# Writing the third group's products of 64 columns into the other two groups' output banks

## The chip, the cores and the metric

The kernel runs on one core of one Trainium2 chip. The metric is the device time of one execution in microseconds, from its first to its last instruction. Four compute engines work on their own queues: TensorE (PE, with its weight loads listed as PEld), VectorE (DVE), ScalarE (ACT) and GpSimd (POOL). SyncE (SP) issues the transfers. Each queue is executed in order, and a semaphore holds an instruction until what it needs is there.

## The reference, cut to what matters

Two layers over 1024 tokens of width 1024: a gated linear attention layer, then a layer in which 8 query heads attend over one shared set of keys and values in three groups. A group is a window and a dilation; the three results are mixed by a softmax over their log sums, gated with `silu(g)`, and projected.

```python
SWA_GROUPS = ((128, 1), (512, 4), (2048, 16))
for gi, (window, dilation) in enumerate(SWA_GROUPS):
    o_g, lse_g = dilated_window_attention(q[:, :, gi], k_sh[:, :, gi], v_sh[:, :, gi], window, dilation)
wts = jax.nn.softmax(jnp.stack(lses, axis=0), axis=0)
o = jnp.sum(wts[..., None] * jnp.stack(outs, axis=0), axis=0)
x = layer_norm(DEEPNORM_ALPHA * x + (o * jax.nn.silu(g)) @ w_out)
```

With dilation 16 and 1024 tokens, the third group splits the tokens into 16 residues of 64 tokens each, and each residue attends only within itself. The change concerns the last step of this group: probabilities times values, and the sum with the other two groups.

## The kernel before, in words

The kernel is written against a recording layer. Every call such as `S.tensor.matmul` is recorded (`record`, line 162), and `order` (line 254) then plays a list schedule: at each step it takes, over all engines, the recorded operation that could start earliest, with ties going to the order of the program. The durations it plays with come from its own function `cost` (lines 543 to 595). They set the order in which instructions stand in the queues and nothing else. For a TensorE product of plain float32 that function has these lines:

```python
        if n >= 128:
            return 4 * n / 2400 + 0.009
        if args[1].shape[0] == 64:
            return 0.12
        m = args[1].shape[1]
        return {32: 0.02, 64: 0.05}.get(m, 0.43)
```

`n` is the number of output columns and `m` that of the weights. Since all instructions are issued in one place, the profile gives line 452 for nearly all of them, and one goes by the names of the tiles.

The second layer (`layer_b`, line 1176) works on 8 units, one query head each. For a unit `u`, `q_proj` makes the queries of the three groups, `scores` makes masked scores (tile `lv`), exponentials (`P`) and their row sums, `g_proj` makes the gate (`sg`), `attend` multiplies with the values, and `close` applies the gate and stores the result `og`. Between the units' instructions stand those of the projections (tile `acc`: three products of 512 columns for each of 8 blocks of the contraction). Units 0 to 3 have their gate before `attend` and are closed right after it; units 4 to 6 are closed later, after `g_proj` at line 1531; unit 7 has its gate first and is attended last, while the output projection already runs.

In `attend`, every probability tile `P` is scaled by the mixing weights `cw`. Then, for the third group, four transposes go to a tile `ms` (4 blocks of 128x128), and four copies put 64x64 blocks into two block-diagonal tiles `diag` (lines 1457 to 1461). Eight products of 128 columns (value block as weights, `diag` block moving) fill two PSUM tiles named `po`. Four copies of DVE bring these in token order into `og`. Two more `po` tiles, from the same two buffers, then take the products of the second group (12) and the first (15), whose probabilities `turn` transposes and masks (tiles `PT`, four buffers); an output element of the second group steps by 4 columns. Two additions bring `po` and `og` together.

TensorE in plain float32 needs two instructions for one product here: the profile counts 128 matmuls and 128 weight loads for the 64 products `po<-diag,V` of the 8 units. PSUM has two buffers each for `acc`, `lv`, `ms` and `po`.

Of the kernel before, what the change touches and what calls it, by code (L numbers as in the profile page):

```python
# [7 lines left out]
F32 = mybir.dt.float32  # L8
# [589 lines left out]
def trunk(tc, xT, wP, wA, wA12, wAv3, w2, wO, wK, wV0, wV12, wB, wOB, par_d,  # L598
          ident_d, lmask_d, cos_d, sin_d, bmask_d, rmask_d, tri_d, lnr_d, out):
    S = Sched(tc, lat=LAT, pad=PAD)  # L600
# [4 lines left out]
    ps = S.pool("ps", space="PSUM")  # L605
# [12 lines left out]
    def page(pool, dt, name):  # L618
        return pool.tile([128, T], dt, name=name, tag="pg", bufs=16)

    def hs(half):
        return slice(half * 512, half * 512 + 512)
# [65 lines left out]
    def blk(x, j):  # L688
        return x[:, j * 128:j * 128 + 128]
# [363 lines left out]
    def small(name, tag, bufs, dt=F32, shape=(128, 512)):  # L1053
        return hp.tile(list(shape), dt, name=name, tag=tag, bufs=bufs)
# [121 lines left out]
    def layer_b(xs, early):  # L1176
# [117 lines left out]
        U = [dict() for _ in range(8)]  # L1294
# [5 lines left out]
        def column(g, j):  # L1300
            return 8 + j % 2 * 4 + j // 2 if g == 1 else g * 8 + j
# [19 lines left out]
        def pieces(P, g, j0):  # L1321
            p, o = P[g, j0 + 1]
            n = 1 if g or not j0 else 2
            v = p[:, o + 256 - n * 256:o + 256].rearrange("p (a two b) -> p a two b", a=n, two=2)
            return v[:, :, 0], v[:, :, 1]
# [89 lines left out]
        def attend(u):  # L1415
            P, cw, Vc = U[u]["P"], U[u]["cw"], V[u // 4]
            og = page(p0, F32, "og")
            U[u]["og"] = og

            def turn(g, j0):  # L1420

                own, prev = (small("PT", "d", 4).rearrange("p (a b) -> p a b", a=4) for _ in range(2))
                pt = ps.tile([128, 4, 128], F32, name="ms", bufs=2)
                def has(x):
                    return x.rearrange("p (a two) b -> p a two b", two=2)[:, :, 1] if g else x[:, 0 if j0 else 1:]

                with S.group():
                    for i in range(4):
                        p, o = P[g, j0 + i]
                        S.tensor.transpose(pt[:, i, :], blk(p[:, o:], BL[g][j0 + i][2] // 128 - 1), ident)  # L1430

                for i in (0, 2):
                    front = pieces(P, g, j0 + i)[0]
                    n = front.shape[1]
                    S.vp.tensor_mul(prev[:, i + 2 - n:i + 2], front, ident[:, None, :].to_broadcast([128, n, 128]))
                S.vector.tensor_mul(own, pt, upto.to_broadcast([128, 4, 128]))
                S.vector.copy_predicated(has(prev), below.to_broadcast(list(has(prev).shape)), has(pt))
                return own, prev


            x = P[2, 0][0].rearrange("p (j k q) -> p k j q", j=4, k=2)
            w = cw[:, 16:24].rearrange("p (k j one) -> p k j one", k=2, j=4)
            S.vector.tensor_mul(x, x, w.to_broadcast([128, 2, 4, 64]))
            for g in (1, 0):
                for j in range(8):
                    p, o = P[g, j]
                    x = p[:, o:o + BL[g][j][2]]
                    S.vap.scale(x, x, cw[:, column(g, j):column(g, j) + 1])

            p = P[2, 0][0]
            pt = ps.tile([128, 4, 128], F32, name="ms", bufs=2)
            with S.group():
                for i in range(4):
                    S.tensor.transpose(pt[:, i, :], blk(p, i), ident)
            for k in range(2):
                h = slice(k * 64, k * 64 + 64)
                for s in range(2):
                    (S.scalar.copy if s else S.vector.tensor_copy)(  # L1460
                        diag[s][h].rearrange("p (j k q) -> p j k q", j=4, k=2)[:, :, k, :], pt[h, :, s * 64:s * 64 + 64])
            po = [ps.tile([128, 512], F32, name="po", bufs=2) for _ in range(2)]
            with S.group():
                for s in range(2):
                    for j in range(4):
                        x = s * 4 + j
                        S.tensor.matmul(po[s][:, j * 128:j * 128 + 128], blk(Vc[2], x), blk(diag[s], j),
                                         start=True, stop=True)
            for s in range(2):
                for k in range(2):  # L1470
                    x = s * 8 + k * 4
                    S.vector.tensor_copy(
                        og.rearrange("p (n a e) -> p n a e", n=8, a=8)[:, :, :, x:x + 4],
                        po[s].rearrange("p (j k a n) -> p k n a j", j=4, k=2, a=8)[:, k])
            po = [ps.tile([128, 512], F32, name="po", bufs=2) for _ in range(2)]
            started = [False, False]

            def pv(bank, outv, vblk, rhs, last=False):
                S.tensor.matmul(outv, vblk, rhs, start=not started[bank], stop=last)
                started[bank] = True  # L1480


            for r0 in (0, 2):
                own, prev = turn(1, 2 * r0)
                for r in (r0, r0 + 1):
                    i = 2 * (r - r0)
                    ov = [po[i].rearrange("p (i r) -> p r i", r=4)[:, r, :] for i in range(2)]
                    pv(0, ov[0], blk(Vc[1], 2 * r), own[:, i, :])
                    pv(1, ov[1], blk(Vc[1], 2 * r), prev[:, i + 1, :])
                    pv(1, ov[1], blk(Vc[1], 2 * r + 1), own[:, i + 1, :])  # L1490

            for n0 in (0, 4):
                own, prev = turn(0, n0)
                for i in range(4):
                    n = n0 + i
                    out_n = po[n // 4][:, i * 128:i * 128 + 128]
                    if n:
                        pv(n // 4, out_n, blk(Vc[0], n - 1), prev[:, i, :])
                    pv(n // 4, out_n, blk(Vc[0], n), own[:, i, :], last=(i == 3))

            for i in range(2):
                S.vector.tensor_add(og[:, hs(i)], po[i], og[:, hs(i)])

        def close(u):
            og, sg = U[u]["og"], U[u]["sg"]
            for i in range(2):
                S.vector.scalar_tensor_tensor(og[:, hs(i)], og[:, hs(i)], 0.5, sg[:, hs(i)],
                                              op0=OP.mult, op1=OP.mult)
            if u < 6:
                S.sync.dma_start(ogB[u], og)  # L1510

        diag = [small("diag", "a", 13) for _ in range(2)]
# [3 lines left out]
        for u in range(8):  # L1516
            scores(u)
            if u < 4:
                g_proj(u)
            if u + 1 < 8:  # L1520
                q_proj(u + 1)
            if u < 7:
                attend(u)
                if u < 4:
                    close(u)
            if u == 3:
                reload_kv()
        for u in (4, 5, 6, 7):
            if u == 7:
                early()  # L1530
            g_proj(u)
            if u < 7:
                close(u)
        attend(7)
        close(7)
        return U

# [29 lines left out]
    U = layer_b(x1s, early)  # L1567
# [118 lines left out]
```

## Time and profile before

| | before |
|---|---|
| three runs, median (lowest to highest) | 1153.4 us (1152.9 to 1153.89) |
| profiled execution: span, the only time its page gives | 1152.7 us |
| PE, PEld busy | 1142.8 us, 975.2 us |
| DVE, ACT, POOL busy | 820.3, 449.1, 188.0 us |
| matmuls and weight loads | 7780 and 7780 |
| granted TensorE clock | 0.998 |

The profiled execution lies 0.7 us below the median of the runs. A row of a group gives its shape, the count, the busy time, the mean of one, and the idle time of the engine ahead of it with what ended most of it. A row of the timeline gives start, length, the engine, and how many instructions of one name follow each other. The length of a matmul in the profile contains a pipeline latency, so what a matmul costs a busy TensorE is the distance from one start to the next.

### The profile page before, as it was taken

To read this page: it belongs to the slowest core of one execution; us is meant where nothing else is said; L and a number is where in the kernel's file an instruction comes from. 1 tells how busy PE (TensorE), PEld (TensorE's weight loads), DVE (VectorE), ACT (ScalarE), POOL (GpSimd) and SP (SyncE) were. 2 spreads that over 40 slices of the span, in tenths; PEclk is the share of its full clock that TensorE was granted. 3 is DMA by queue.
4 is the path that set the end of the run, shared out by engine and by line. 5 is a ranking of instruction groups with operands and counts; after the bars stand their busy time and mean duration, and the time that the engine had idled before them with its cause. 6 is when DMAs were issued, how large, how long until landed. Compare 5 with 4: busy or idle time off the path is not lost.

```text
span 1152.7 us, 19731 instructions
## 1 busy us (share of the span) xinstructions
PE 1142.8 (99%) x7780; PEld 975.2 (85%) x7780; DVE 820.3 (71%) x1634; ACT 449.1 (39%) x929; POOL 188.0 (16%) x139
## 2 busy tenths in 40 slices
PE   9999999999999999999999999999999999999997
PEld 9888888889988888888988888888888888888876
DVE  6286862786966699764366868686777878767678
ACT  5355431646463335311214242424222443444342
POOL 1000100112011120211020303030211312212200
PEclk9999999999999999999999999999999999999999
DMA  7211222111144365443611111121141111134544
GB/s 256 71 38 38 74 79 87 38 61 51 57 171 140 137 214 158 166 143 103 208 47 34 51 38 57 38 50 45 38 165 39 38 21 38 39 96 126 193 136 182
DMA packets 93372, 108.39 MB, mean 94 GB/s; under 512 B 43648, under 2 KB 61952, under 8 KB 93280
## 3 DMA queue, kind: packets, MB, share of 16 engines
q1 hardware_dynamic: 93280, 107.13, 29.6%
q8 instruction: 61, 1.00, 0.4%
q14 instruction: 31, 0.25, 0.1%
HBM read 85.94 MB, written 21.17 MB: 93 GB/s over the span
## 4 chain that ended last, share of the span: by engine, by line
PE 93%; DVE 4%; DMA 2%; ACT 1%; issue 1%; POOL 0%; DVEq 0%; ACTq 0%
PE acc L452 63%; PE po L452 9%; PE lv L452 8%; PE vac L452 7%; PE ms L452 4%; PE pro L452 2%; DMA wf<-in_wOB 2%; DVE rt L452 1%; DVE wl L452 1%; DVE x1l L452 0%; ACT wh L452 0%; DVE P L452 0%; DVE lnA L452 0%; ACT woh L452 0%; DVE wol L452 0%
## 5 line engine op out<-in xcount | busy, mean ns | idle before, releaser
L452 PE MATMUL acc<-x1h,wh 128*128 128x512 f32 x608 | 252.3, 415 | 0.0
L452 PE MATMUL acc<-x1h,wl 128*128 128x512 f32 x608 | 237.6, 391 | 0.0
L452 PE MATMUL acc<-x1l,wh 128*128 128x512 f32 x608 | 237.1, 390 | 0.0
L452 ACT ACTIVATE wh<-wf 128x1024 fp32r<-128x1024 f32 (+2 forms) x104 | 108.1, 1040 | 281.0 <-PE acc L452 194.8
L452 POOL TENSOR_TENSOR wl<-wf,wh 128x1024 fp32r<-128x1024 f32 x39 | 93.5, 2397 | 553.1 <-ACT wh L452 414.8
L452 ACT ACTIVATE P<-P,sts 128x128 f32<-128x128 f32 (+2 forms) x192 | 81.5, 426 | 139.6 <-DVE sts L452 139.3
L452 PEld LDWEIGHTS acc<-x1h,wl 128*128 128x128 f32 x608 | 114.1, 188 | 24.5
L452 PEld LDWEIGHTS acc<-x1l,wh 128*128 128x128 f32 x608 | 114.5, 188 | 21.3
L452 PEld LDWEIGHTS acc<-x1h,wh 128*128 128x128 f32 x608 | 114.4, 188 | 21.1
L452 DVE TENSOR_TENSOR wl<-wf,wh 128x1024 fp32r<-128x1024 f32 (+2 forms) x66 | 83.4, 1265 | 58.2 <-ACT wh L452 48.0
L452 PE MATMUL acc<-xh,wh 128*128 128x512 f32 x256 | 101.8, 397 | 0.0
L452 PE MATMUL acc<-xh,wl 128*128 128x512 f32 x256 | 99.8, 390 | 0.0
L452 PE MATMUL acc<-xl,wh 128*128 128x512 f32 x256 | 99.7, 390 | 0.0
L452 DVE TENSOR_TENSOR t<-acc,cosT 128x512 f32<-128x512 f32 x60 | 41.4, 689 | 65.7 <-PE acc L452 65.7
L452 DVE TENSOR_TENSOR t<-acc,sinT 64x512 f32<-64x512 f32 x120 | 82.5, 688 | 1.6
L452 PE MATMUL lv<-K,Q 128*64 128x64 f32 (+2 forms) x512 | 70.2, 286 | 0.0
L452 DVE CUSTOM_DVE_ANT_0 P<-lv,bmask 128x256 f32<-128x256 f32 (+1 forms) x128 | 46.7, 379 | 25.1 <-PE lv L452 23.7
L452 PEld LDWEIGHTS lv<-K,Q 128*128 128x128 f32 (+1 forms) x512 | 53.8, 163 | 10.0 <-issue 1.6
L452 PE MATMUL acc<-ogh,wh 128*128 128x512 f32 x152 | 60.1, 395 | 0.0
L452 PE MATMUL acc<-ogh,wl 128*128 128x512 f32 x152 | 59.2, 389 | 0.0
L452 PE MATMUL acc<-ogl,wh 128*128 128x512 f32 x152 | 59.2, 389 | 0.0
L452 PEld LDWEIGHTS acc<-xh,wl 128*128 128x128 f32 x256 | 48.0, 188 | 10.2
(252 smaller groups left out, 2233.4 us busy)
## 6 DMA issues: line engine op xcount, KB each, us to landing
wf<-in_wB SPq DMA_DIRECT2D x32, 512.0 KB
wf<-in_wA SPq DMA_DIRECT2D x24, 512.0 KB
wf<-in_wO SPq DMA_DIRECT2D x16, 512.0 KB
wf<-in_wOB SPq DMA_DIRECT2D x16, 512.0 KB
wf<-in_wV SPq DMA_DIRECT2D x12, 512.0 KB
res<-in_xT SPq DMA_DIRECT2D x16, 256.0 KB
x1d<-rt SPq DMA_DIRECT2D x16, 256.0 KB
out<-rt SPq DMA_DIRECT2D x16, 256.0 KB
```

The costliest lines, as they stand in the source:

```text
L452: getattr(handle[o.eng], meth)(*[conv(a) for a in args], **{k: conv(v) for k, v in kw.items()})
```

## The change: what it does

The two `po` tiles are allocated once per unit. Each product of the third group is split by token halves, so that 16 products of 64 columns take the place of 8 of 128, and each writes straight to the places of its tokens in the bank that the other two groups add into. The output of one product has three strides: 2 residues 4 columns apart, 8 places 16 columns apart, and 4 blocks 128 columns apart, the last varying fastest. The first of these products starts the bank; all later ones add. The four copies from `po` to `og` and the two additions are gone. `close` reads `po` where the gate is there already (units 0 to 3 and 7); in units 4 to 6 two copies on ACT bring `po` to `og` first.

```diff
             po = [ps.tile([128, 512], F32, name="po", bufs=2) for _ in range(2)]
-            with S.group():
-                for s in range(2):
-                    for j in range(4):
-                        x = s * 4 + j
-                        S.tensor.matmul(po[s][:, j * 128:j * 128 + 128], blk(Vc[2], x), blk(diag[s], j),
-                                         start=True, stop=True)
-            for s in range(2):
-                for k in range(2):
-                    x = s * 8 + k * 4
-                    S.vector.tensor_copy(
-                        og.rearrange("p (n a e) -> p n a e", n=8, a=8)[:, :, :, x:x + 4],
-                        po[s].rearrange("p (j k a n) -> p k n a j", j=4, k=2, a=8)[:, k])
-            po = [ps.tile([128, 512], F32, name="po", bufs=2) for _ in range(2)]
             started = [False, False]
...
+            with S.group():
+                for i in range(2):
+                    ov = po[i].rearrange("p (n a s k j) -> p s j k a n", n=4, a=8, s=2, k=2)
+                    for s in range(2):
+                        for j in range(4):
+                            d = blk(diag[s], j).rearrange("p (k a n) -> p k a n", k=2, a=8)
+                            pv(i, ov[:, s, j], blk(Vc[2], s * 4 + j), d[:, :, :, i * 4:i * 4 + 4])
...
-            for i in range(2):
-                S.vector.tensor_add(og[:, hs(i)], po[i], og[:, hs(i)])
+            if "sg" not in U[u]:
+                for i in range(2):
+                    S.scalar.copy(og[:, hs(i)], po[i])
+                po = None
+            U[u]["po"] = po
...
-                S.vector.scalar_tensor_tensor(og[:, hs(i)], og[:, hs(i)], 0.5, sg[:, hs(i)],
+                S.vector.scalar_tensor_tensor(og[:, hs(i)], po[i] if po else og[:, hs(i)], 0.5, sg[:, hs(i)],
```

Over the whole program TensorE has 128 products of 64 columns for 64 of 128, and otherwise the same ones; DVE has 32 copies `og<-po` and 16 additions less; ACT has 6 copies `og<-po` more; the number of transfers is the same. The planner's `cost` takes its branch for fewer than 128 columns, so it books 0.43 for each of the 16 products where it booked 0.222 for each of the 8. From the first such group on, the order of the queues is therefore another.

The first place is TensorE in unit 0, from the third group's products on (`po<-diag,V`). The transposes `ms` that follow are those of the next turns; `lv<-K,Q 64x64` are scores of the next unit. Before:

```order
L452 MATMUL po<-diag,V_5481 128x128 x8
L452 MATMUL ms<-ident,P 128x128 x8
L452 MATMUL lv<-K_5174,Q 64x64 x16
L452 MATMUL po<-PT,V_5401 128x128 x2
L452 MATMUL lv<-K_5008,Q 128x128
L452 MATMUL po<-PT,V_5401 128x128 x10
L452 MATMUL ms<-ident,P 128x128 x4
```

With the change, same place:

```order
L452 MATMUL po<-diag,V_5481 128x2x8x4 x16
L452 MATMUL po<-PT,V_5401 128x128 x6
L452 MATMUL ms<-ident,P 128x128 x8
L452 MATMUL lv<-K_5174,Q 64x64 x16
L452 MATMUL lv<-K_5008,Q 128x128
L452 MATMUL acc<-x1h_4373,wh 128x512
L452 MATMUL acc<-x1l_4390,wh 128x512
L452 MATMUL acc<-x1h_4373,wl 128x512
L452 MATMUL po<-PT,V_5401 128x128 x6
L452 MATMUL po<-PT,V_4656 128x128 x7
```

The first six products of the second group now stand directly behind those of the third, ahead of the transposes and scores.

The second place is TensorE in unit 5. Before, six triples of `acc` and two pairs of `lv` stood between the third group's products and the eight transposes; with the change:

```order
L452 MATMUL acc<-x1h_4351,wh 128x512
L452 MATMUL acc<-x1l_4362,wh 128x512
L452 MATMUL acc<-x1h_4351,wl 128x512
L452 MATMUL po<-diag,V_7898 128x2x8x4 x16
L452 MATMUL ms<-ident,P 128x128 x8
L452 MATMUL lv<-K_7888,Q 64x64 x16
L452 MATMUL lv<-K_7886,Q 128x128
L452 MATMUL acc<-x1h_4373,wh 128x512
L452 MATMUL acc<-x1l_4390,wh 128x512
L452 MATMUL acc<-x1h_4373,wl 128x512
L452 MATMUL po<-PT,V_7896 128x128 x12
```

The transposes of the second group's probabilities now follow the products at once; the projection's triples are ahead of the products instead.

The third place is DVE in the same unit with the change, from the scaling of the third group's tile on. `TENSOR_SCALAR P<-P,cw` scales the first and second groups' tiles, which those eight transposes read.

```order
L452 TENSOR_TENSOR P<-P,cw 128x2x4x64
L452 TENSOR_TENSOR t_8764<-acc,cosT 128x512
L452 TENSOR_TENSOR t_8771<-acc,sinT 64x512 x2
L452 COPY diag<-ms 64x4x64 x2
L452 TENSOR_TENSOR Q<-t_8764,t_8771 128x4x8x16
L452 TENSOR_SCALAR P<-P,cw 128x128
L452 TENSOR_SCALAR P<-P,cw 128x256 x5
L452 TENSOR_SCALAR P<-P,cw 128x128 x3
L452 TENSOR_SCALAR P<-P,cw 128x256
L452 TENSOR_TENSOR PT<-P,ident 128x128 x2
L452 TENSOR_TENSOR PT<-ms,upto 128x512
L452 COPY_PREDICATED PT<-below,ms 128x2x128
```

Before, the four copies `og<-po` stood ahead of the scalings, of which DVE had seven; now the copies are gone and DVE has ten.

More of the change, by code (lines that the diff above doesn't have):

```diff
@@ L1499, in attend, with close @@
                     pv(n // 4, out_n, blk(Vc[0], n), own[:, i, :], last=(i == 3))
-            for i in range(2):
-                S.vector.tensor_add(og[:, hs(i)], po[i], og[:, hs(i)])
-        def close(u):
-            og, sg = U[u]["og"], U[u]["sg"]
-            for i in range(2):
-                S.vector.scalar_tensor_tensor(og[:, hs(i)], og[:, hs(i)], 0.5, sg[:, hs(i)],
+            if "sg" not in U[u]:
[3 more added lines that the diff above has]
+            U[u]["po"] = po
+        def close(u):
+            og, sg, po = (U[u][n] for n in ("og", "sg", "po"))
+            for i in range(2):
+                S.vector.scalar_tensor_tensor(og[:, hs(i)], po[i] if po else og[:, hs(i)], 0.5, sg[:, hs(i)],
                                               op0=OP.mult, op1=OP.mult)
```

## The prediction, made before the run

> **What bounds the kernel now.** First the page's head and its chain of waits, then what TensorE waited for in all.
>
> ```profile
> span 1152.7 us, 19731 instructions
> PE 1142.8 (99%) x7780; PEld 975.2 (85%) x7780; DVE 820.3 (71%) x1634; ACT 449.1 (39%) x929; POOL 188.0 (16%) x139
> PE 93%; DVE 4%; DMA 2%; ACT 1%; issue 1%; POOL 0%; DVEq 0%; ACTq 0%
> PE pro L452 <- DVE Dg L452: 1.2, 1, 1.2
> PE po L452 <- DVE PT L452: 0.8, 1, 0.8
> PE ms L452 <- DVE sum L452: 0.5, 2, 0.2
> PE ms L452 <- ACT sum L452: 0.2, 1, 0.2
> ```
>
> TensorE is busy 99% of the span and 93% of the chain. The last four lines are all its waits (total, times, longest): 2.7 us, of which 0.8 lies in the stage of the change. So the 820 us of DVE are hidden: work taken from DVE can win back those 0.8 us and no more, and each microsecond put on TensorE lengthens the kernel. The stretches of units 0 and 5, in the columns stretch, PE, PEld, DVE, ACT, POOL, clock, DMA:
>
> ```profile
> 654.80:715.70 60.90, 60.90 (x347) 52.30 (x346) 45.23 (x119) 21.36 (x68) 13.14 (x12) 1.00 0.17 45
> 946.00:996.00 50.00, 50.00 (x307) 43.27 (x306) 40.32 (x122) 21.45 (x77) 13.46 (x11) 1.00 0.16 34
> ```
>
> In unit 0 DVE has 15.7 us to spare, in unit 5 only 9.7. TensorE is without a gap in both, at full clock, and DMA does little.
>
> **What the change removes.**
>
> ```profile
> L452 DVE COPY og<-po 128x256 f32<-128x256 f32 x32 | 11.8, 418 | 2.1 <-PE po L452 1.5
> L452 DVE TENSOR_TENSOR og<-po,og 128x512 f32<-128x512 f32 x16 | 11.0, 690 | 6.0 <-PE po L452 5.9
> L452 ACT ACTIVATE th<-acc 128x512 f32<-128x512 f32 x16 | 9.4, 588 | 20.6 <-PE acc L452 20.6
> ```
>
> DVE loses 11.8 us of copies and 11.0 us of additions; ACT gains 6 copies of 512 columns at about 0.59 us (third row, same size and source), 3.5 us on an engine 39% busy. Behind TensorE's queue this is worth nothing, with one exception in unit 7:
>
> ```profile
> 1052.89 1.40 DVE L452 COPY og<-po 128x256 f32<-128x256 f32 x4
> 1054.95 3.13 PE L452 MATMUL po<-PT,V 128*128 128x128 f32 x24 [0.77 <-DVE PT L452]
> ```
>
> There the four copies stand ahead of the masks that TensorE waits 0.77 us for. Without them this gap closes: -0.8 us.
>
> **What it adds to TensorE.** The 64 products become 128 of half the columns: the same 8192 columns, twice the instructions and weight loads.
>
> ```profile
> 654.83 1.95 PE L452 MATMUL po<-diag,V 128*128 128x128 f32 x16
> 656.61 1.04 PE L452 MATMUL ms<-ident,P 128*128 128x128 f32 x8
> 657.58 1.15 PE L452 MATMUL lv<-K,Q 128*64 128x64 f32 x32
> 658.66 0.71 PE L452 MATMUL po<-PT,V 128*128 128x128 f32 x4
> ```
>
> From 654.83 to 656.61 the 16 instructions of the 8 products take 1.78 us, 0.111 each. No row shows a full set of weights followed by only 64 columns, so that price has to be bounded. Streaming alone gives half of 0.111, 0.056. The 64-column scores have 64 weight columns and alternate between the two halves of the array: 32 in 1.08 us (657.58 to 658.66), 16 per half, 0.067 each. What speaks for more is the weight load:
>
> ```profile
> L452 PEld LDWEIGHTS lv<-X 128*32 128x32 f32 x1536 | 16.5, 110 | 3.0 <-issue 2.8
> L452 PEld LDWEIGHTS lv<-K,Q 128*64 128x64 f32 x256 | 8.1, 138 | 2.3 <-issue 1.6 <-DVE zz L452 0.7
> L452 PEld LDWEIGHTS po<-diag,V 128*128 128x128 f32 x128 | 15.4, 191 | 0.7 <-issue 0.2
> L452 PE MATMUL po<-PT,V x432: 270/275/377, 658.7 to 1065.5; 128*128 128x128 f32 x144
> ```
>
> Load lengths grow with the weight columns, 110, 138, 191 ns for 32, 64, 128: from 64 to 128 that is 53 ns for 64 columns, so 128 columns take about 107. The last row says the same from the other side: a `po` product is 270 ns at least, and 377 at most. The longest is the one at 658.66 that finds its weights not loaded (the load starts with it): 107 ns more. So two such loads can't follow each other closer than about 107 ns, and while the load of one product can run under another of 128 columns (both about 107, hence 0.111), it can't hide under 53 ns of streaming. I take 0.111 for the new instruction too: a product of 64 columns costs what one of 128 does. The ends are 0.056 and, if load and streaming did not overlap at all, 107 + 53 = 0.160.
>
> Sum: 32 x 0.111 = 3.56 us per unit for 1.78, +1.78, and +14.2 us over 8 units, all on the bounding engine. The ends give 1.79 us (+0.1 in all) and 5.12 us (+27).
>
> The strided output is the other unknown. The second group writes with steps of 4 columns, the first without:
>
> ```profile
> 659.43 2.40 PE L452 MATMUL po<-PT,V 128*128 128x128 f32 x20
> 664.39 3.29 PE L452 MATMUL po<-PT,V 128*128 128x128 f32 x28
> ```
>
> Without the 0.275 of the last one, 19 steps take 2.13 us and 27 take 3.02: 0.112 each. A step of 4 costs nothing; one of 128 is not shown, but half the columns in the same 0.111 leave it twice the time per column. I take nothing. [...]
>
> **What the new order adds.** In unit 0, TensorE goes from the third group straight to six products of the second. Their masked tile is the one made by
>
> ```profile
> 654.35 0.45 DVE L452 COPY_PREDICATED PT<-below,ms 128x256 f32<-128x256 uint8 x1
> ```
>
> done at 654.80, while TensorE gets there at 654.83 + 3.56 = 658.4. The later steps follow alike: transposes until 659.7 + 0.9, masks 1.1 us behind the first four of them at 661.4, wanted (after 16 score products, one more and a triple) at 662.6. Units 0 to 3 have slack. Units 4 to 6 have less. Unit 5 before:
>
> ```profile
> 943.97 0.60 PE L452 MATMUL ms<-ident,P 128*128 128x128 f32 x4
> 946.47 1.95 PE L452 MATMUL po<-diag,V 128*128 128x128 f32 x16
> 953.70 1.03 PE L452 MATMUL ms<-ident,P 128*128 128x128 f32 x8
> 946.67 0.69 DVE L452 TENSOR_TENSOR t<-acc,cosT 128x512 f32<-128x512 f32 x1 [0.16 <-PE acc L452]
> 947.38 1.39 DVE L452 TENSOR_TENSOR t<-acc,sinT 64x512 f32<-64x512 f32 x2
> 950.68 1.13 DVE L452 TENSOR_TENSOR Q<-t,t 128x512 f32<-128x512 f32 x1
> 951.74 3.25 DVE L452 TENSOR_SCALAR P<-P,cw 128x128 f32<-128x128 f32 x7
> 648.37 1.16 DVE L452 TENSOR_SCALAR P<-P,cw 128x128 f32<-128x128 f32 x5
> ```
>
> The eight transposes came 7.2 us behind the third group's products, with projections between; now they stand directly behind. Count from the four transposes (943.97 here, call it 0): 0.4 for them, five triples of 0.68 and 3.56 bring TensorE to the eight transposes at 7.3. DVE must have scaled their sources by then: 0.3 until the projection's last product is through, 0.69 + 1.39 for its rotation, 0.86 for two copies to `diag` (0.43 each), 1.1 for `Q`, then ten scalings at 0.46 (the row of seven) or 0.23 (the row of five): 9.0 or 6.6. TensorE waits 1.7 us or not at all; I take 0.8. Unit 6 has the same order, unit 4 one triple less and a DVE queue as full: 3 x 0.8 = +2.4 us, between 0 and 5.1. Behind those transposes stand the next unit's scores, so nothing else fills the wait.
>
> Total: 14.2 + 2.4 - 0.8 = +15.8, a span of 1168.5 us. The runs' median lies 0.7 above the span before: **1169 us**, +1.4%.
>
> **The rivals.**
>
> *The load hides after all, and DVE's relief counts.* If the array takes a new load while the last is still waiting, an instruction costs 0.056 to 0.067: 1.79 to 2.14 us per unit, +0.1 to +2.9 in all. If DVE, free of the copies, also scales at 0.23 in units 4 to 6, no wait appears, and with -0.8 the kernel is not slower: 1152.7 to 1155.5, say 1154. For it: three lengths of weight loads are latencies, and loads do run in pairs in the 64-column scores. Against it: the 377. It decides up to 0.058 per instruction: 8 x (32 x 0.058 - 1.78) = +0.6. [...]
>
> *The load hides, but the order makes TensorE wait.* At 2 us for the products TensorE reaches the eight transposes at 5.8, DVE at 6.6 to 9.0 as before: 0.8 to 3.2, 2 us in each of three units, +6, with +1.5 for the products and -0.8: 1160.
>
> *Short runs or wide steps cost.* The moving block is read in runs of 4 columns, the output written 128 apart. At 0.160 per instruction: +27 - 0.8, without waits since TensorE is late: 1180; more if it is worse. For it: no row has these patterns. Against it: the step of 4 that cost nothing.
>
> **How the numbers follow.** Load-bound, as summed: 68%; its own range is 1165 (no waits: 14.2 - 0.8, or 0.109 per instruction) to 1174 (5.1 of waits and as much again in unit 7). Hidden load with waits 14%, hidden without 8%, wide steps 10%. Two in ten left out gives 1157 to 1178. This kernel can't be told from no change within 0.2%, 2.3 us. Faster needs the second case and more than 0.8 us from elsewhere, which the 2.7 us of waits hardly hold: 2%. Within 0.2%: most of the hidden load without waits, 6%. Slower: 92%.
>
> **What would show it.** Right: the groups of 32 instructions `po<-diag,V` take 3.5 to 3.6 us from first start to the next instruction, weight loads 107 to 112 ns apart; units 0 to 3 last 62.7 instead of 60.9 us; the waits of PE name `ms` or `po` behind DVE's `P` or `PT` with 0 to 5 us; the 0.77 of unit 7 is gone; DVE has some 20 us less. Wrong: a group of 1.8 to 2.1 us (the load hides), or of 5 us and more (steps cost); waits in units 0 to 3, or over 2 us in a unit.

## The result and the profile after

The changed kernel takes 1167.9 us (1167.71 to 1168.49) against 1153.64 us (1152.9 to 1155.78) for the kernel before, run beside it: a ratio of 1.0122, with a 95% interval of 1.0108 to 1.0137. It is slower by 14.3 us. First the head of the page after, with its chain of waits, and all waits of TensorE (total, times, longest):

```profile
span 1166.7 us, 19927 instructions
PE 1157.0 (99%) x7908; PEld 991.6 (85%) x7908; DVE 799.7 (69%) x1602; ACT 449.2 (38%) x929; POOL 175.0 (15%) x129
PE 96%; DVE 3%; ACT 1%; issue 0%; DVEq 0%; ACTq 0%
PE pro L452 <- DVE Dg L452: 1.2, 1, 1.2
PE ms L452 <- ACT P L452: 0.5, 1, 0.5
PE ms L452 <- DVE sum L452: 0.2, 1, 0.2
PE ms L452 <- ACT sum L452: 0.2, 1, 0.2
```

The span grew by 14.0 us and TensorE's busy time by 14.2 (1142.8 to 1157.0). DVE lost 20.6 us (820.3 to 799.7) and POOL 13.0 (188.0 to 175.0; the planner moved some of its work to DVE), and nothing of that shortened the span: TensorE was already busy 99% of it. Its waits went from 2.7 to 2.1 us. The timeline of TensorE in unit 0, from the third group's products on, and the stretches from one such group to the next (stretch, PE, PEld, DVE, ACT, POOL, clock, DMA):

```profile
655.48 3.68 PE L452 MATMUL po<-diag,V 128*128 128x64 f32 x32
659.00 1.56 PE L452 MATMUL po<-PT,V 128*128 128x128 f32 x12
655.48:718.22 62.74, 62.74 (x363) 54.16 (x362) 42.43 (x113) 20.91 (x68) 13.21 (x12) 1.00 0.17 44
718.22:780.96 62.74, 62.74 (x363) 54.15 (x362) 42.40 (x113) 21.03 (x68) 13.19 (x12) 1.00 0.17 44
```

The 32 instructions take 3.51 us (655.48 to 659.00), where 16 took 1.78: +1.73 us. Units 0 and 1 last 62.74 us each; the stretch shown of before lasted 60.90. So of the 1.84 us that a unit lost, 1.73 are the products. Eight groups make +13.9 us (from the starts before rounding). The clock is 1.00, and TensorE has no gap.

### The profile page after: what moved, and what is told of

Its sections match the earlier page's. It is cut to its first block, busy times and chain, and to the rows that moved or that the text cites. A ratio compares the mean times of both kernels' runs of the same rounds, so it can differ in the third digit from the quotient of the medians.

```text
span 1166.7 us, 19927 instructions
## 1 busy us (share of the span) xinstructions
PE 1157.0 (99%) x7908; PEld 991.6 (85%) x7908; DVE 799.7 (69%) x1602; ACT 449.2 (38%) x929; POOL 175.0 (15%) x129
## 4 chain that ended last, share of the span: by engine, by line
PE 96%; DVE 3%; ACT 1%; issue 0%; DVEq 0%; ACTq 0%
PE acc L452 63%; PE po L452 10%; PE lv L452 10%; PE vac L452 7%; PE ms L452 4%; PE pro L452 2%; DVE rt L452 1%; DVE wl L452 1%; DVE x1l L452 0%; ACT P L452 0%; DVE lnA L452 0%; ACT wh L452 0%; DVE diag L452 0%; ACT diag L452 0%; DVE sum L452 0%
## 5 line engine op out<-in xcount | busy, mean ns | idle before, releaser
L452 POOL TENSOR_TENSOR wl<-wf,wh 128x1024 fp32r<-128x1024 f32 x38 | 91.1, 2397 | 549.0 <-ACT wh L452 397.0
L452 DVE TENSOR_TENSOR Q<-t,t 128x512 f32<-128x512 f32 x43 | 57.5, 1336 | 1.3
```

The lines of the kernel that those rows point to most:

```text
L452: getattr(handle[o.eng], meth)(*[conv(a) for a in args], **{k: conv(v) for k, v in kw.items()})
```

## The experiments

Three questions were open: what sets the price of a narrow product, what the new order costs, and what the relief of DVE is worth. The first had three theories: the weight load of 128 columns, the steps and short runs of the new pattern, or a fixed price per instruction.

### The split alone, in place

```diff
-    S.tensor.matmul(po[s][:, j * 128:j * 128 + 128], blk(Vc[2], x), blk(diag[s], j), ...)
+    for c in (j * 128, j * 128 + 64):
+        S.tensor.matmul(po[s][:, c:c + 64], blk(Vc[2], x), diag[s][:, c:c + 64], ...)
```

The planner's booking of the halves was halved too, so that the queues keep the order of before.

> The kernel before, with one thing changed: each product of the third group is made as two of 64 adjacent columns into adjacent columns of the bank it wrote before. The copies, the additions and the order of the queues stay, and there is no step in any output. Load theory (an instruction costs the load of 128 weight columns, 0.110 us, whatever it streams up to 128 columns): the 32 instructions of a unit take 3.5 us instead of 1.78, +1.73 x 8 = +13.8, time 1167.4 us, and the wait of 0.77 us in unit 7 stays. Pattern theory (64 columns stream in 0.055 us, and only the runs of 4 columns and the steps of 4, 16 and 128 of the changed kernel made it 0.110): 32 x 0.055 = 1.8 us a unit, time 1153.5 us.

Measured: 1167.73 us, ratio 1.0124 (1.0107 to 1.0140). Its timeline of TensorE in unit 0:

```profile
655.27 3.68 PE L452 MATMUL po<-diag,V 128*128 128x64 f32 x32
658.79 1.04 PE L452 MATMUL ms<-ident,P 128*128 128x128 f32 x8
```

Again 3.52 us, with adjacent columns on both sides, copies and additions in place and the old order. The split alone gives the whole loss of the changed kernel; the pattern theory (1153.5) falls. One thing in the expectation was wrong: the wait of unit 7 did not stay. That is taken up below.

### Half as many weight columns

```diff
+    for m in (0, 64):
         ...
-        S.tensor.matmul(po[s][:, c:c + 64], blk(Vc[2], x), diag[s][:, c:c + 64], ...)
+        S.tensor.matmul(po[s][m:m + 64, c:c + 64], Vc[2][:, x * 128 + m:x * 128 + m + 64], diag[s][:, c:c + 64], ...)
```

> As the split in place, but each of the 64-column products is made twice with 64 weight columns each, first all with the lower half of the value columns, then all with the upper half: 64 instructions a unit, each with a load and a stream half as long as before. Load theory: a load of 64 columns is about 54 ns (138 - 191 ns against 128 columns in the profile before), the stream of 64 columns 53 ns, so 0.055 each, 64 x 0.055 = 3.5 us a unit, time again about 1167.4 us. Theory of a fixed price (any instruction of plain float32 needs 0.110 us, and the weights have nothing to do with it): 64 x 0.110 = 7.0 us a unit, +5.25 x 8 = +42, time 1195.5 us.

Measured: 1169.68 us, ratio 1.0143 (1.0127 to 1.0158). Its timeline in unit 0:

```profile
655.28 3.77 PE L452 MATMUL po<-diag,V 128*64 128x64 f32 x64
658.98 1.09 PE L452 MATMUL ms<-ident,P 128*128 128x128 f32 x8
```

Now 64 instructions take 3.70 us, 0.058 each: the same 64 streamed columns cost half when the weights have half the columns. So there is no fixed price of 0.11, which would have given 1195.5 us. The load sets the price. (The expectation had 0.055; the 0.003 more is most of the 2 us above its 1167.4.)

### The same number of instructions with 128, 64 and 32 columns

Three kernels issue 64 instructions per unit in the third group, all with 128 weight columns: `repeat_128` makes each of the old products four times, `repeat_64` each half twice, `quarters` splits into four of 32 columns.

```diff
     # quarters
-    S.tensor.matmul(po[s][:, j * 128:j * 128 + 128], ..., blk(diag[s], j), ...)
+    for c in range(j * 128, j * 128 + 128, 32):
+        S.tensor.matmul(po[s][:, c:c + 32], ..., diag[s][:, c:c + 32], ...)
```

> As the split in place, but into four products of 32 adjacent columns each: 64 instructions a unit with 128 weight columns. Load theory: 64 x 0.110 = 7.0 us a unit, +5.26 x 8 = +42, time 1195.5 us. If streaming and a fixed part made up the price (a fixed 0.057 us and 0.053 for 64 columns would also give the 0.110): 64 x (0.057 + 0.027) = 5.4 us a unit, time 1182 us.

> The split in place, with each product of 64 columns made twice (the second overwrites the first): 64 instructions in a row a unit, as the quarters have, but of 64 columns. In the quarters the granted clock fell to 0.50 after some 6 us of such instructions, and they cost 35 us more than 64 x 0.112. By the load price alone: 64 x 0.111 = 7.1 us a unit, +42.6, 1196 us. If it is the length of a stretch of loads at 0.11 us apart that lowers the clock: as the quarters, 1225 to 1235 us. If it is the narrow stream of 32 columns: 1196 us at full clock.

> The kernel before, with each product of 128 columns made four times: 64 instructions in a row a unit, each with a load and a stream of 107 ns. Load price as for 64 and 32 columns: 7.1 us a unit, 1196 us at full clock. If the length of a stretch of loads lowers the clock whatever is streamed: 1225 to 1235 us. If streaming counted on top of the load: more than 7.1 us a unit at full clock.

Measured: 1195.7 us for `repeat_128`, 1195.67 for `repeat_64` (both 1.0354, 1.0324 to 1.0384), and 1230.24 for `quarters` (1.0662, 1.0642 to 1.0681). Unit 0 of the first two, `repeat_128` first, TensorE's timeline:

```profile
654.51 7.30 PE L452 MATMUL po<-diag,V 128*128 128x128 f32 x64
661.65 1.04 PE L452 MATMUL ms<-ident,P 128*128 128x128 f32 x8
```

```profile
655.31 7.25 PE L452 MATMUL po<-diag,V 128*128 128x64 f32 x64
662.40 1.04 PE L452 MATMUL ms<-ident,P 128*128 128x128 f32 x8
```

7.14 and 7.09 us, 0.111 each: with 128 weight columns an instruction costs the same for 64 and for 128 streamed columns, and the two kernels take the same time. The timeline and stretches of `quarters` in unit 0 (columns as above, the clock third from the end):

```profile
655.07 8.32 PE L452 MATMUL po<-diag,V 128*128 128x32 f32 x64
663.20 1.95 PE L452 MATMUL ms<-ident,P 128*128 128x128 f32 x8
657.00:659.00 2.00, 2.00 (x20) 2.00 (x20) 0.24 (x1) 0.00 (x0) 0.00 (x0) 1.00 0.04 12
659.00:661.00 2.00, 2.00 (x20) 2.00 (x19) 0.51 (x2) 0.00 (x0) 0.00 (x0) 0.99 0.00 0
661.00:663.00 2.00, 2.00 (x12) 2.00 (x12) 0.00 (x0) 0.00 (x0) 0.00 (x0) 0.50 0.00 0
667.00:668.00 1.00, 1.00 (x7) 1.00 (x6) 0.38 (x4) 0.63 (x4) 0.00 (x0) 0.61 0.00 0
668.00:669.00 1.00, 1.00 (x11) 1.00 (x10) 0.00 (x0) 0.14 (x2) 0.00 (x0) 1.00 0.00 0
```

At full clock (657 to 661) a stretch of 2 us counts 20 instructions, among them the one or two that reach in over each edge: 18 x 0.111 us, with 32 columns as well. A price made of a fixed part and the columns would have been 0.084, 24 instructions. Then the granted clock falls to 0.50, from 661 on, and a stretch of 2 us counts 12. That is why the kernel came out 35 us above the 1195.5 expected by the load price: its mean clock is 0.969 where the kernel before has 0.998, and 0.029 of a span of 1227 us is 36 us. `repeat_64` and `repeat_128` pass 7.09 and 7.14 us of such loads in unit 0 at a clock of 1.00, so it isn't the length; more of it in the last section.

### A wide product between the narrow ones

```diff
     pv(i, ov[:, s, j], blk(Vc[2], s * 4 + j), d[:, :, :, i * 4:i * 4 + 4])
+    S.tensor.matmul(wide, blk(xs[0][0], j), xs[0][0][:, 0:512], start=True, stop=True)
```

> The changed kernel with one more product behind each product of the third group: 512 columns of fast float32, one instruction, into a bank that nobody reads, 16 a unit. It asks whether weight loads can run further ahead than one instruction. A wide one takes 0.227 us alone. If the array holds one load ahead and no more, a narrow pair still costs 2 x 0.110, since the load behind each narrow stream has only that stream to hide under: 16 x (0.22 + 0.227) = 7.2 us a unit for the 48 instructions, +29 on the changed kernel, 1197 us. If loads can run two ahead, the wide stream covers the loads of the pair behind it: 16 x (2 x 0.055 + 0.227) = 5.4 us a unit, 1183 us, and narrow products cost nothing between wide ones.

Measured: 1197.78 us, one execution. Its timeline of TensorE:

```profile
655.76 0.33 PE L452 MATMUL po<-diag,V 128*128 128x64 f32 x2
655.90 0.48 PE L452 MATMUL ms<-x1h 128*128 128x512 f32 x1
656.21 0.33 PE L452 MATMUL po<-diag,V 128*128 128x64 f32 x2
```

A round takes 0.45 us, which is 2 x 0.112 + 0.227: nothing is won. Inside it the time lies elsewhere. The narrow pair passes in 0.14 us (655.76 to 655.90), less than two loads of 0.11, and the wide one then takes 0.31 (655.90 to 656.21) instead of 0.227. That fits a first narrow load made under the wide stream, and a wide product whose own load had only a narrow stream to hide under. The profile after shows the same limit: the load of the first narrow product starts at 655.26, with the wide one ahead of it, and the next load not before 655.49, when that narrow product has begun (655.48). One load runs ahead, not two.

### The same weights twice in succession

```diff
-    for i in range(2):
-        for s in range(2):
-            for j in range(4):
+    for s in range(2):
+        for j in range(4):
+            for i in range(2):
```

> The changed kernel with the same products in another order within each group of sixteen: the two token halves of one value block follow each other, so two products in succession have the same weights. The rest of every queue is the same. Load theory, every instruction loading its weights anew: 3.51 us a unit and 1167.9 us as before. If the array kept weights that it already holds, or a repeated load were cheaper: at best 16 of the 32 instructions of a unit at 0.055, 2.6 us a unit, 1160.8 us.

Measured: 1168.65 us, ratio 1.0120 (1.0090 to 1.0149). Unit 0:

```profile
655.17 3.68 PE L452 MATMUL po<-diag,V 128*128 128x64 f32 x32
658.68 1.56 PE L452 MATMUL po<-PT,V 128*128 128x128 f32 x12
```

3.51 us as before: a product pays its two loads also when the product ahead of it had the same weights. The runs do not show whether the two instructions of one product load the same numbers, so whether the array ever found its own weights again stays open.

### Steps in the output at full width

```diff
-    S.tensor.matmul(po[s][:, j * 128:j * 128 + 128], blk(Vc[2], x), blk(diag[s], j), ...)
+    S.tensor.matmul(po[s].rearrange("p (n a k j) -> p j k a n", n=8, a=8, k=2)[:, j],
+                    blk(Vc[2], x), blk(diag[s], j).rearrange("p (k a n) -> p k a n", k=2, a=8), ...)
```

> The kernel before, its 64 products of 128 columns kept whole, but each written with steps into its own bank (2 residues 4 columns apart, 8 places 8 apart, 8 blocks 64 apart, the last varying fastest) from a moving block read in the same order (steps of 1 in runs of 8); the four copies read accordingly. Here streaming and load take the same 107 ns, so nothing hides a slower read or write. If steps in PSUM and short runs cost nothing: 1.78 us a unit, 1153.4 us. [...]

Measured: 1154.02 us, ratio 1.0002 (0.9993 to 1.0011). Unit 0:

```profile
655.68 1.95 PE L452 MATMUL po<-diag,V 128*128 128x128 f32 x16
657.46 1.04 PE L452 MATMUL ms<-ident,P 128*128 128x128 f32 x8
```

1.78 us, to the hundredth as before, with steps of 4, 8 and 64 columns. Where streaming is not hidden under a longer load, steps in the output cost nothing here. The changed kernel's own steps of 4, 16 and 128 were run only under the longer load: 3.51 us with them, 3.52 in place.

### The order and the planner's booking

```diff
         if n >= 128:
             return 4 * n / 2400 + 0.009
+        if n in (32, 64) and args[1].shape[1] == 128 and args[1].shape[0] == 128:
+            return 4 * 128 / 2400 + 0.009
```

> The changed kernel, with only the planner's booking of a 64-column product set to what it takes (0.222 us for the two instructions instead of 0.43). The instructions are the same, the order differs from unit 4 on. If the order of the changed kernel costs only the one gap of 0.65 us ahead of the transposes of unit 4, this gives at best 1167.9 - 0.7 = 1167.2 us. If the order costs more than the waits show (for example by projections at a worse price behind it), 1165 us or less. The products stay at 3.51 us a unit in both.

Measured: 1169.02 us, ratio 1.0139 (1.0124 to 1.0155), so neither number. The gap in unit 4 went, and another of the same size came in unit 6; the line of its waits:

```profile
PE po L452 <- DVE PT L452: 0.6, 1, 0.6
```

The time of this order is not below that of the changed kernel, whose order the wrong booking made. The 14 us do not come from the order.

### DVE's relief, and the wait of unit 7

Two kernels keep the 64 wide products. `no_copies` leaves out the copies and additions, and with them the third group's part of the output:

```diff
-    for s in range(2):
-        for k in range(2):
-            S.vector.tensor_copy(og..., po[s]...)
...
-    for i in range(2):
-        S.vector.tensor_add(og[:, hs(i)], po[i], og[:, hs(i)])
```

> The relief of DVE alone: the kernel before with its 64 products of 128 columns, but without the four copies and the two additions of a unit; the other two groups' bank is closed as in the changed kernel, and the third group's part is left out of the output. If DVE's work is hidden but for the 0.77 us of unit 7: 1153.5 - 0.8 = 1152.7 us, and at least 20 us less of DVE. If DVE's work costs TensorE more than its waits show: 1150 us or less.

`copies_on_act` only moves unit 7's copies (the planner then orders a few instructions of that unit otherwise):

```diff
-    S.vector.tensor_copy(
+    (S.scalar.copy if u == 7 else S.vector.tensor_copy)(
```

> The kernel before, with the four copies of the third group's banks in unit 7 alone made on ACT instead of DVE, so that the masks which TensorE waits 0.77 us for have no copies ahead of them. No product is split. If that wait ends with the copies: 1153.4 - 0.8 = 1152.7 us, a ratio of 0.9993. If another wait takes its place at once (the planner also moves products in that unit): 1153.4 us or a little more.

Measured: 1153.76 us for `no_copies`, ratio 1.0002 (0.9993 to 1.0012), and 1153.81 us for `copies_on_act`, ratio 1.0003 (0.9994 to 1.0011). The heads of their profiled executions, `no_copies` first, and its one wait for a `po` product:

```profile
span 1151.6 us, 19663 instructions
PE 1141.9 (99%) x7780; PEld 975.7 (85%) x7780; DVE 805.9 (70%) x1612; ACT 451.0 (39%) x932; POOL 169.2 (15%) x116
PE po L452 <- DVE diag L452: 0.2, 1, 0.2
```

```profile
span 1151.8 us, 19731 instructions
```

Both spans are about 1 us shorter than the 1152.7 of before, and the 0.77 us is gone from both. But 21 executions of the kernel before, run beside `copies_on_act`, have spans from 1150.9 to 1153.4, so two profiled spans cannot settle 1 us. The medians do not show it: 0.8 us is 0.07%, and the intervals reach from -0.07% to +0.12%. Neither version can be told from the kernel before. DVE shrank by 14.4 us rather than the 20 expected of `no_copies`, as the planner gives DVE other work (POOL has 18.8 us less).

And the wait went away in the split in place too, where the four copies are still on DVE. Its DVE timeline in unit 7, and under it the row of the same scalings before:

```profile
1062.14 2.18 DVE L452 TENSOR_SCALAR P<-P,cw 128x256 f32<-128x256 f32 x8
1064.24 0.74 DVE L452 COPY og<-po 128x256 f32<-128x256 f32 x2
1065.14 0.76 DVE L452 COPY og<-po 128x256 f32<-128x256 f32 x2 [0.16 <-PE po L452]
```

```profile
1049.32 3.65 DVE L452 TENSOR_SCALAR P<-P,cw 128x256 f32<-128x256 f32 x8
```

There the products last 1.7 us longer, and the eight scalings ahead of the copies took 2.18 us instead of 3.65, so DVE waits for TensorE and not the other way round. Without the copies the wait was gone, but they were not the only thing that could end it.

What made the same scalings take 0.46 or 0.27 us each is seen in POOL. First the last of the eight scalings before and POOL's work around it, then POOL's in the split in place:

```profile
1051.60 1.37 DVE L452 TENSOR_SCALAR P<-P,cw 128x256 f32<-128x256 f32 x1
1050.59 0.94 POOL L452 TENSOR_TENSOR PT<-P,ident 128x128 f32<-128x128 f32 x2 [2.34 <-DVE P L452]
1051.49 1.33 POOL L452 TENSOR_TENSOR ogl<-ogf,ogh 128x512 fp32r<-128x512 f32 x1
```

```profile
1063.41 1.64 POOL L452 TENSOR_TENSOR PT<-P,ident 128x128 f32<-128x128 f32 x2 [2.35 <-DVE P L452]
```

Before, that one scaling began 0.11 us after a POOL instruction of 1.33 us and lasted as long as it. It held up the copies by about 1.0 us, more than the wait. In the profiles before and after, a scaling of 256 columns that met no POOL instruction took 0.33 to 0.35 us, and every one that took longer (0.49 to 0.58, one of them 1.37) overlapped one. In the split in place, with the queues in the same order, it was POOL that took longer (1.64 us instead of 0.94) and no scaling did. So the two engines seem to hold each other up. That is read from the traces; no run took POOL's work away.

## Why the prediction was right, step by step

- **What bounds the kernel.** Right. DVE's relief (20.6 us here, 14.4 in `no_copies`) was worth no more than the one wait of 0.8 us, and not even that shows in a median.
- **The price of a narrow instruction.** Right, and the largest term: 0.111 forecast, 3.56 us a unit; measured 3.51 us, because the first load of a group hides under the wide projection ahead of it (it starts at 655.26, the group at 655.48). +13.9 us against the +14.2 of the sum. The reasoning from the one product of 377 ns and from load lengths of 110, 138 and 191 ns held: the runs with 32, 64 and 128 columns, and with 64 weight columns, leave the load as the only one of the causes weighed. It was 0.111 us per instruction with 128 weight columns and 0.058 with 64.
- **The strided output at nothing.** Right; now shown at full width for steps of 4, 8 and 64 (1.78 us), and for the change's own steps no loss beside the load (3.51 us with them, 3.52 in place).
- **The wait in units 4 to 6: +2.4 us.** Mis-sized; 0.5 us measured, once. The step that failed is "ten scalings at 0.46 (the row of seven) or 0.23 (the row of five)"; the forecast took about the mean of the two waits that these give, 1.7 us and none. TensorE and DVE in unit 5 after:

```profile
947.87 3.68 PE L452 MATMUL po<-diag,V 128*128 128x64 f32 x32
951.39 1.04 PE L452 MATMUL ms<-ident,P 128*128 128x128 f32 x8
948.31 2.42 DVE L452 TENSOR_SCALAR P<-P,cw 128x128 f32<-128x128 f32 x10
```

TensorE reached the eight transposes 7.4 us after the four (943.98), as forecast (7.3). DVE was through at 950.73, 6.8 us after them: the ten scalings took 0.24 us each on average, the low end, and nobody waited. They began at 948.31, 4.3 us after the four transposes, as summed; only their own length was off. The 0.46 was a mean that held a scaling beside POOL: of the seven in unit 5 before, one lasted 1.31 us, across the end of a POOL multiplication of 1.75:

```profile
951.74 1.31 DVE L452 TENSOR_SCALAR P<-P,cw 128x128 f32<-128x128 f32 x1
951.22 1.75 POOL L452 TENSOR_TENSOR Q<-t,t 128x512 f32<-128x512 f32 x1
```

In the changed kernel POOL did nothing during the ten scalings but for the last 0.04 us; its next instruction began at 950.69. In unit 4 TensorE did wait, but for ACT, which the prediction did not look at:

```profile
905.55 1.35 PE L452 MATMUL ms<-ident,P 128*128 128x128 f32 x8 [0.48 <-ACT P L452]
903.53 0.38 ACT L452 ACTIVATE P<-P,sts 128x128 f32<-128x128 f32 x1
903.92 2.38 ACT L452 ACTIVATE P<-P,cw 128x256 f32<-128x256 f32 x6
```

ACT began its six scalings at 903.92, straight behind exponentials of the next unit, and ended at 906.3.

- **The wait of unit 7: -0.8 us.** It went in the profile after, as said; but the split in place shows that the copies were not its only condition: the scaling beside POOL, by its length, was another.
- **The sum.** 13.9 + 0.5 - 0.8 = 13.6 from the measured terms, against 15.8 forecast and a span longer by 14.0; the remaining 0.4 is not placed (units 0 and 1 lost 0.1 us each beside the products). The forecast span was 1.8 us too long, 1.9 of it the waits that did not come and 0.3 the products, less the 0.4; the median lay 1.2 above the span instead of 0.7 (which says only where the profiled execution lies among the runs), so the median of 1167.9 is 1.1 below the forecast. The low end given for the load-bound case, 1165, does not come out of its terms: 1153.4 + 14.2 - 0.8 is 1166.8, and 1166.3 with 0.109. The measured time lies above either.
- **The rivals.** A hidden load (1154 or 1160) is excluded by `wide_between` and by the 3.51 us; steps or short runs (1180) by `strided_128` and the split in place.

## What to carry to other kernels

On a busy TensorE, count plain float32 products in instructions: with 128 weight columns two of them cost 0.22 us here for 128 and for 64 streamed columns, and for 32 as long as the clock was 1.00, so a product should not be split for the sake of where its output lands. A copy on an engine with slack was cheaper here than a second weight load (nothing that a median shows, against 1.73 us a unit), even when it looks like pure overhead; first ask whether the engine that is relieved is ever the one waited for. When a trace has no row for a new shape, its longest and shortest instances of a neighbour (270 and 377 ns here) tell what is hidden under what. And a row's mean is not a price until one has seen what ran beside its longest instance.

## What the hardware showed unexpectedly

With 32 columns streamed for every load of 128 weight columns, the granted clock fell to 0.50 after some 6 us of such products in unit 0, and stayed there for 6.8 us, until about 667.8 (0.61 is the mean of 667 to 668), through the transposes and scores behind them. In units 1, 4 and 5 it was 0.76, 0.67 and 0.75 over the products. The stretch that holds the products and the one behind them in unit 0 of `quarters`, its products in units 1 and 5, and then the first stretch in `repeat_64`:

```profile
655.00:663.20 8.20, 8.20 (x66) 8.16 (x65) 1.63 (x5) 0.00 (x0) 0.53 (x1) 0.86 0.21 66
663.20:670.00 6.80, 6.80 (x64) 6.35 (x65) 2.95 (x12) 0.77 (x4) 0.91 (x2) 0.66 0.00 0
724.50:733.70 9.20, 9.20 (x65) 9.18 (x64) 1.57 (x4) 0.00 (x0) 0.48 (x1) 0.76 0.17 57
994.30:1003.60 9.30, 9.30 (x66) 9.30 (x64) 2.84 (x7) 3.99 (x15) 3.57 (x2) 0.75 0.20 58
```

```profile
655.00:663.20 8.20, 8.20 (x75) 8.12 (x73) 2.48 (x7) 0.00 (x0) 0.78 (x1) 1.00 0.20 66
```

The rows call TensorE busy all the time in both, so a busy PE in the profile is not what the clock goes by. By the load price alone `quarters` would have cost 8 x (64 x 0.111 - 1.78) = 42.6 us; it cost 76.7, so the lowered clock cost another 34 us. With 64 and 128 columns and the same spacing the clock was 1.00 in unit 0, and 0.999 and 0.998 over the whole span. That suggests the share of time in which columns stream as the cause, by estimate at most about a half at 64 columns and a quarter at 32 (of 0.111 us, from the 0.058 that 64 columns took with their load in `narrow_weights`); it was not tested apart from that.
